# Layer 0's last half group of the down projection by block products, and a later place for the last square root's preparation

## The chip, the cores and the metric

The kernel runs on one core of a Trainium2 chip. Times are device microseconds (us) of one execution of the whole program. The engines are called as in the profile: PE (matrix multiplication; PEld are its weight loads), DVE (the vector engine), ACT (the activation engine), POOL, and SP, which here only issues DMAs.

## The reference

Two layers of a decoder trunk over 512 positions with a width of 1024. Each layer mixes (attention, convolution and RWKV heads between an input and an output projection) and then has a squared-ReLU MLP. The change lies in the MLP of layer 0 and in the end of the MLP of layer 1:

```python
D_MODEL = 1024; SEQ = 512; DEPTH = 2; D_FF = 4 * D_MODEL

def rms_norm(x, g):
    y = x * lax.rsqrt(jnp.mean(x * x, axis=-1, keepdims=True) + NORM_EPS)
    return y * g

for l in range(DEPTH):
    h = rms_norm(x, norm_mix_g[l])
    ...                                   # mixing, ends in x = x + mixed @ w_out[l]
    h = rms_norm(x, norm_mlp_g[l])
    x = x + jnp.square(jax.nn.relu(h @ w_mlp_up[l])) @ w_mlp_down[l]
return rms_norm(x, final_norm_g)
```

## The kernel before

**Layout.** x is kept transposed in eight tiles x[0] to x[7] of 128 x 512 (features on partitions, positions along the row). Every product is made in three passes: each operand is split into a rounded part (hi) and a remainder (lo), and hi x hi, hi x lo and lo x hi are summed. The hi part is a cast on ACT, the lo part a subtraction on DVE (lines 348 and 349 for weights of a plain product, 1583 and 1584 for those of a block product).

**The MLP.** It has 32 hidden tiles of 128 x 512, kept as pairs (hi, lo) in `mids` by `kept()` (lines 1406 to 1414), in two rings `mh` and `ml` of ten places each. The first four come from plain products (`up`), the other 28 from 14 calls of `two()`, each of which makes two hidden tiles by a block scheme. The down projection takes the hidden tiles in groups h = 0 to 7 of four, and each group in two halves of four output tiles: `down(h, range(0, 4))` and `down(h, range(4, 8))`. In the loop of lines 1694 to 1701 one half group follows each `two()`, so that it lags behind; after the loop the halves of group 6 are done and the two halves of group 7 are left, which lines 1702 to 1704 do with no `two()` between them.

**The two ways of a half group.** `down()` (lines 1659 to 1683) asks the list `DN_QUADS` (line 184), by layer, of pairs (h, half).

- Plain: for each of the four output tiles j, 4 hidden tiles x 3 passes = 12 matmuls of 512 columns into one accumulator, then one addition into x[j]. The weights of j are one load of 256 KB, one cast and one lo part. In layer 0 the group h = 7 then calls `norm_tile(j)` for j < 6, which accumulates the squares of x[j] for the next layer's norm (a square on ACT, line 384; from j = 1 on an addition into `accm` on DVE, line 385).
- Block products, `quad()` (lines 1577 to 1657): the four output tiles are taken as two pairs (j, j + 1). The weights of a pair are seen as 2 x 2 blocks (output tile j or j + 1, even or odd hidden tile), the hidden tiles as 2 x 2 blocks (even or odd tile, left or right half of the positions), and the product is made with seven block products in place of eight, each of 2 hidden tiles x 3 passes = 6 matmuls of 256 columns, 84 for the half group. For this, sums and differences of weights (lines 1618 to 1622) and of hidden tiles are needed, and the results are combined (lines 1638 to 1657). Products on accumulators pa, pb, pc appear in the profile as qa, qb and qc. The seven are issued in steps: first the two of the unsummed weights `w0` for both pairs, then the two of `s12`, then the two of `s34`, and at last the one of `w22`.

The sums of hidden tiles are made by `turn_blocks(h, k, b1, b2)` (lines 1560 to 1575), once for each two hidden tiles of a group (k = 0, 1): four differences on DVE, a cast on ACT and a lo part on DVE for two of them, then two smaller casts and lo parts for the other two. It is called in the loop right after the half group of that round (lines 1699 to 1701), and only for groups of which `DN_QUADS` has a half. It writes the tiles `dhi` and `dlo` of its k, and the right halves of `acts[2k]` and `acts[2k + 1]`, the MLP's input tiles (ahif, alof in the profile), which nothing else reads any more. All groups share these places, so in layer 0, whose list has both halves of the groups 2, 4 and 6, the groups between them go plain (group 1 has one half by block products).

**Buffers.** Weights of plain products and the unsummed ones of block products share the tags `raw`, `whi` and `wlo` with three places each, taken in turn (`Pool`, lines 243 to 257). The sums of weights go through the tiles s2 and s4 (one place each) and `shi`, `slo` (five each). The tag `c0` (two places) holds both the intermediate tiles of `turn_blocks` and the results c0 of `quad`.

**Order of the work.** The mixing stage of each layer is issued in an order written out by hand (`ORDER`). In the MLP, the order of instructions on each engine is set at compile time by a scheduler, from the order of the program and from what is ready; each engine then runs its own list in order. Layer 1's written order begins with products of its input projection (pj), which read the scaled tiles of x (ahim, alom; made for j < 6 by `scaled`, lines 391 and 392, and for the last two by `entry`, lines 426 and 427), and then has pssm, small matmuls that sum the accumulated squares `accm` over the features.

**The end of the kernel.** In layer 1 the last group goes through `last_group()` (lines 473 to 569), which also makes the final norm. Its root is a Sqrt activation (line 511). Line 480 issues a small Sqrt on a constant column, which makes ACT load its table.

Of the kernel before, what the change touches and what calls it, by code (L numbers as in the profile page):

```python
# [10 lines left out]
F32 = mybir.dt.float32  # L11
F32R = mybir.dt.float32r
# [168 lines left out]

N_ONE = 4

DN_QUADS = (((1, 0), (2, 0), (2, 1), (4, 0), (4, 1), (6, 0), (6, 1)), ((1, 0), (2, 0), (2, 1), (4, 0), (4, 1), (6, 0), (6, 1)))

WHOLE = 2
PT = 1
# [86 lines left out]
def tile_trunk(ctx: ExitStack, tc: tile.TileContext, xT, wts, prm_d, cst_d, lora_d, gup_d, lam_d, fin_d, hd_d, out):  # L274
# [198 lines left out]
    def last_group(fp, wbase, mids):  # L473
# [3 lines left out]
        mine = mids[-4:]  # L477
        acc = wp.tile([P, S], F32, tag="acc", bufs=1, name="accF")

        act.activation(cp.tile([P, NB], F32, tag="rr", bufs=2, name="rrF")[:, :1], ones1, AF.Sqrt)  # L480

        def group(j, home=None):
            return weights(wbase + NG_IN + NG_OUT + NG_UP + 8 * g + j, 4, NK, home=home)
# [87 lines left out]
    for l in range(L):  # L571
# [826 lines left out]
        with ExitStack() as mx:  # L1398
# [161 lines left out]
            def turn_blocks(h, k, b1, b2):  # L1560

                a = fp.tile([P, 2, H], F32, tag="c0", bufs=2, name=f"ta{l}_{h}_{k}")
                b = fp.tile([P, 2, H], F32, tag="c0", bufs=2, name=f"tb{l}_{h}_{k}")
                dve.tensor_tensor(a[:, 0], b1[:, H:], b1[:, :H], ALU.subtract)
                dve.tensor_tensor(a[:, 1], b2[:, H:], a[:, 0], ALU.subtract)
                dve.tensor_tensor(b[:, 0], b2[:, H:], b1[:, H:], ALU.subtract)
                dve.tensor_tensor(b[:, 1], b2[:, :H], a[:, 1], ALU.subtract)
                hi, lo = [fp.tile([P, 2, H], F32R, tag=f"d{p}{k}", name=f"d{p}{l}_{h}_{k}") for p in ("hi", "lo")]
                act.copy(hi, a)
                dve.tensor_tensor(lo, a, hi.bitcast(F32), ALU.subtract)  # L1570
                for i in range(2):
                    turned[i, k] = hi[:, i], lo[:, i]
                    vhi, vlo = turned[2 + i, k] = [t[:, H:] for t in acts[2 * k + i]]
                    act.copy(vhi, b[:, i])
                    dve.tensor_tensor(vlo, b[:, i], vhi.bitcast(F32), ALU.subtract)

            def quad(h, half):
# [15 lines left out]
                        pe.matmul(pt, wlo, ahi, start=False, stop=last and i == 1, skip_group_check=True)  # L1593

                blk = lambda d, q: lambda i: [t[:, q * H:(q + 1) * H] for t in mids[4 * h + 2 * i + d]]
                trn = lambda q: lambda i: turned[q, i]

                def add(j, q, pt):
                    dve.tensor_tensor(x[j][:, q], pt, x[j][:, q], ALU.add)
# [28 lines left out]
                for step in ((0, 1), (2, 3), (5, 4), (6,)):  # L1628
                    for j, w0, s12, s34, w22, (pa, pb, pc) in ab:
                        n = f"{l}_{h}_{j}"  # L1630
                        for c in step:
# [7 lines left out]
                            elif c == 2:  # L1639
                                product(pb, s12, (0, 1), trn(0), True, False)  # L1640
                                keep["p5", j] = copied("p5", pb, n)
                            elif c == 3:
                                product(pa, s12, (2, 3), trn(1), False, False)
                                keep["u2", j] = copied("u2", pa, n)
                            elif c == 5:
                                product(pb, s34, (2, 3), blk(1, 1), False, True)
                                c0 = keep["c0", j]
                                dve.tensor_tensor(c0[:, right], pb, keep["u2", j], ALU.add)
                                add(j, slice(0, S), c0)
                            elif c == 4:  # L1650
                                product(pa, s34, (0, 1), trn(2), False, False)
                                c1 = copied("c1", pa, n)
                                dve.tensor_tensor(c1, c1, keep["p5", j], ALU.add)  # L1653
                                add(j + 1, right, c1)
                            else:
                                product(pa, w22, (0, 1), trn(3), False, True)
                                add(j + 1, left, pa)

            def down(h, js):

# [115 lines left out]
```

## Time and profile before

| | us |
|---|---|
| median of 3 runs | 1225.97 |
| lowest and highest of them | 1225.78, 1226.85 |
| the profiled execution | 1225.8 |
| its span, from first to last instruction | 1224.0 |
| PE busy in it | 1213.5 |
| DVE busy | 1038.7 |
| ACT busy | 765.2 |
| POOL busy | 307.0 |

Times within the profile count from the start of the span. The stage around the change, layer 0's last block product to layer 1's first norm sums, lies between about 560 and 620 us. In rows of the timeline the columns are start, length, engine, line, operation, output and inputs, shapes and count; what stands in square brackets is the time that the engine was idle before, and what it waited for. Records of one engine can overlap by some 0.1 us, since an instruction starts before the last has quite ended.

### The profile page before, as it was taken

The numbers are of one execution on the slowest core, as the hardware profiler recorded it, in microseconds if no ns is written. First come the engines' busy times: TensorE is split into PE (matmuls) and PEld (weight loads), VectorE is DVE, ScalarE is ACT, GpSimd is POOL, SyncE is SP. The second block draws the span as 40 slices with busy tenths as digits, with TensorE's granted clock in tenths as the row PEclk, the third lists the DMA queues.
The fourth block names the chain that finished last, engine by engine and source line by source line (L and its number), as shares of the span: only waits on it lengthen the run. The fifth ranks groups of instructions, "written<-read, shape, count | busy, mean of one in ns | idle before, by whom it ended". The sixth has DMA issues, their size and how long they took to land.

```text
span 1224.0 us, 27303 instructions
## 1 busy us (share of the span) xinstructions
PE 1213.5 (99%) x10242; PEld 1070.0 (87%) x10242; DVE 1038.7 (85%) x2214; ACT 765.2 (63%) x1678; POOL 307.0 (25%) x446
## 2 busy tenths in 40 slices
PE   9999999999999999999999999999999999999997
PEld 7888788888999999989888888888889999999997
DVE  6787888878899998989866777887798999899895
ACT  7785655558476655646575656464675666465565
POOL 2364636341100010000026455464211000101001
PEclk9999999999999999999999999999999999999999
DMA  6533334126645473631235243232455556546112
GB/s 222 163 94 96 114 88 112 54 86 181 164 125 161 129 188 96 184 86 53 78 114 160 84 128 113 88 82 71 151 152 150 142 133 169 138 130 180 54 54 86
DMA packets 95508, 148.51 MB, mean 121 GB/s; under 512 B 22544, under 2 KB 26384, under 8 KB 95376
## 3 DMA queue, kind: packets, MB, share of 16 engines
q1 hardware_dynamic: 87168, 132.39, 34.5%
q0 software_dynamic: 7488, 13.63, 7.4%
q8 instruction: 80, 1.31, 0.4%
q10 hardware_dynamic: 720, 0.75, 0.2%
q14 instruction: 52, 0.43, 0.1%
HBM read 137.56 MB, written 9.18 MB: 120 GB/s over the span
## 4 chain that ended last, share of the span: by engine, by line
PE 92%; DVE 4%; ACT 2%; issue 1%; DMA 1%; POOL 0%; SPq 0%; POOLq 0%; ACTq 0%; DVEq 0%
PE pj L287 23%; PE dn L287 14%; PE pa L287 13%; PE po L287 8%; PE qa L287 7%; PE pb L287 7%; PE pc L287 3%; PE qb L287 3%; PE qc L287 2%; PE dnF L287 2%; PE sc L287 1%; PE ptt L292 1%; PE pg L287 1%; PE pyy L287 1%; DVE tlo L1469 1%
## 5 line engine op out<-in xcount | busy, mean ns | idle before, releaser
L697 POOL TENSOR_TENSOR wlo<-raw,whi 128x512 fp32r<-128x512 f32 x84 | 112.4, 1338 | 261.5 <-ACT whi L685 228.1
L287 PE MATMUL pj<-ahim,whi 128*128 128x512 f32 x392 | 156.9, 400 | 0.0
L287 PE MATMUL pj<-ahim,wlo 128*128 128x512 f32 x392 | 156.6, 399 | 0.0
L287 PE MATMUL pj<-alom,whi 128*128 128x512 f32 x392 | 156.0, 398 | 0.0
L1480 POOL DMA_DIRECT2D s<-wts x52 | 45.7, 879 | 433.1 <-DVE c1q L1653 52.8
L685 ACT CAST whi<-raw 128x512 fp32r<-128x512 f32 x142 | 87.7, 618 | 72.3 <-PE pj L287 24.5
L1494 ACT CAST shi_p<-s 128x512 fp32r<-128x512 f32 x112 | 69.6, 622 | 51.8 <-PE pa L287 29.8
L287 PE MATMUL dn<-ml,whi 128*128 128x512 f32 x256 | 99.9, 391 | 0.4 <-DVE ml L1413 0.4
L287 PE MATMUL dn<-mh,whi 128*128 128x512 f32 x256 | 99.9, 391 | 0.0
L287 PE MATMUL dn<-mh,wlo 128*128 128x512 f32 x256 | 99.3, 390 | 0.0
L287 PE MATMUL pa<-thi,shi_p 128*128 128x256 f32 x336 | 95.2, 283 | 0.0
L287 PE MATMUL pa<-tlo,shi_p 128*128 128x256 f32 x336 | 94.8, 282 | 0.0
L287 PE MATMUL pa<-thi,slo_p 128*128 128x256 f32 x336 | 94.3, 281 | 0.0
L1495 DVE TENSOR_TENSOR slo_p<-s,shi_p 128x512 fp32r<-128x512 f32 x112 | 76.3, 689 | 13.8 <-ACT shi_p L1494 13.0
L287 PEld LDWEIGHTS pj<-alom,whi 128*128 128x128 f32 x392 | 73.9, 189 | 14.0 <-issue 0.5
L287 PEld LDWEIGHTS pj<-ahim,wlo 128*128 128x128 f32 x392 | 73.9, 188 | 13.8 <-issue 0.2
L287 PEld LDWEIGHTS pj<-ahim,whi 128*128 128x128 f32 x392 | 73.9, 189 | 13.6 <-issue 0.3
L1494 ACT CAST shi_p<-raw 128x512 fp32r<-128x512 f32 x84 | 52.0, 621 | 30.5 <-PE pb L287 12.7
L287 PEld LDWEIGHTS pa<-thi,shi_p 128*128 128x128 f32 x336 | 63.0, 187 | 0.9 <-ACT u L1538 0.5
L287 PEld LDWEIGHTS pa<-thi,slo_p 128*128 128x128 f32 x336 | 63.7, 190 | 0.0
L287 PEld LDWEIGHTS pa<-tlo,shi_p 128*128 128x128 f32 x336 | 63.2, 188 | 0.0
L1495 DVE TENSOR_TENSOR slo_p<-raw,shi_p 128x512 fp32r<-128x512 f32 x84 | 57.7, 688 | 5.1 <-ACT shi_p L1494 4.5
(648 smaller groups left out, 4002.2 us busy)
## 6 DMA issues: line engine op xcount, KB each, us to landing
raw<-wts SPq DMA_DIRECT2D x307, 256.0 KB, 3.0
rawq<-wts SPq DMA_DIRECT2D x56, 256.0 KB, 2.9
s<-wts SPq DMA_DIRECT2D x52, 256.0 KB, 3.6
s<-wts POOLq DMA_DIRECT2D x52, 256.0 KB, 4.6
qs<-dqhi SPq DMA_DIRECT2D x24, 128.0 KB, 3.3
ks<-dkhi SPq DMA_DIRECT2D x24, 128.0 KB, 3.5
x<-xT SPq DMA_DIRECT2D x8, 256.0 KB, 5.3
dqhi<-qhi SPq DMA_DIRECT2D x6, 256.0 KB, 3.3
```

The costliest lines, as they stand in the source:

```text
L287: ins = nc.tensor.matmul(*a, **k)
L292: ins = nc.tensor.transpose(*a, **k)
L685: yield act.copy(hi[:, k0:k1], raw[:, k0:k1])
L697: yield eng.tensor_tensor(lo[:, k0:k1], raw[:, k0:k1], hi[:, k0:k1].bitcast(F32), ALU.subtract)
L1469: dve.tensor_tensor(lo[:, u], t, hi[:, u].bitcast(F32), ALU.subtract)
L1480: pool.dma_start(t.rearrange("p k c -> p (k c)"), of[1], accum_op=ALU.add)
L1494: act.copy(hi, src)
L1495: dve.tensor_tensor(lo, src, hi.bitcast(F32), ALU.subtract)
```

## The change

1. `DN_QUADS` of layer 0 gets the pair (7, 0): the first half of the last group goes by block products. The second half, (7, 1), stays plain.
2. With this `turn_blocks` is called for group 7 too, in the last two rounds of the loop. The call for k = 0 comes while `quad(6, 1)` still has to read the sums of group 6. So it gets places of its own: two places of each of the rings mh and ml (`own`, `ring`). The call for k = 1 writes the shared places, behind `quad(6, 1)`. `turned` is indexed by the group as well.
3. `quad()` calls `norm_tile` for the two tiles of a pair after its last product if h is 7.
4. The small Sqrt of `last_group` reads one column of the last hidden tile, which the last `two()` makes, instead of a constant.

```diff
-DN_QUADS = (((1, 0), (2, 0), (2, 1), (4, 0), (4, 1), (6, 0), (6, 1)), ...
+DN_QUADS = (((1, 0), (2, 0), (2, 1), (4, 0), (4, 1), (6, 0), (6, 1), (7, 0)), ...
...
-        act.activation(cp.tile([P, NB], F32, tag="rr", bufs=2, name="rrF")[:, :1], ones1, AF.Sqrt)
+        act.activation(cp.tile([P, NB], F32, tag="rr", bufs=2, name="rrF")[:, :1], mine[-1][0][:, :1].bitcast(F32), AF.Sqrt)
...
-                hi, lo = [fp.tile([P, 2, H], F32R, tag=f"d{p}{k}", name=f"d{p}{l}_{h}_{k}") for p in ("hi", "lo")]
+                ring = lambda n: [fp.tile([P, 2, H], F32R, tag="m" + p[0], bufs=RING, name=f"d{p}{l}_{h}_{k}_{n}") for p in ("hi", "lo")]
+                own = h == 2 * N_KG - 1 and k == 0
+                hi, lo = ring(0) if own else [fp.tile([P, 2, H], F32R, tag=f"d{p}{k}", name=f"d{p}{l}_{h}_{k}") for p in ("hi", "lo")]
+                if own:
+                    more = ring(1)
                 act.copy(hi, a)
                 dve.tensor_tensor(lo, a, hi.bitcast(F32), ALU.subtract)
                 for i in range(2):
-                    turned[i, k] = hi[:, i], lo[:, i]
-                    vhi, vlo = turned[2 + i, k] = [t[:, H:] for t in acts[2 * k + i]]
+                    turned[h, i, k] = hi[:, i], lo[:, i]
+                    vhi, vlo = turned[h, 2 + i, k] = [t[:, i] for t in more] if own else [t[:, H:] for t in acts[2 * k + i]]
...
-                trn = lambda q: lambda i: turned[q, i]
+                trn = lambda q: lambda i: turned[h, q, i]
...
                                 product(pa, w22, (0, 1), trn(3), False, True)
                                 add(j + 1, left, pa)
+                                if h == 2 * N_KG - 1:
+                                    norm_tile(j, f"m{l + 1}")
+                                    norm_tile(j + 1, f"m{l + 1}")
```

More of the change, by code (lines that the diff above doesn't have):

```diff
@@ L182 @@
 N_ONE = 4
-DN_QUADS = (((1, 0), (2, 0), (2, 1), (4, 0), (4, 1), (6, 0), (6, 1)), ((1, 0), (2, 0), (2, 1), (4, 0), (4, 1), (6, 0), (6, 1)))
+DN_QUADS = (((1, 0), (2, 0), (2, 1), (4, 0), (4, 1), (6, 0), (6, 1), (7, 0)), ((1, 0), (2, 0), (2, 1), (4, 0), (4, 1), (6, 0), (6, 1)))
 WHOLE = 2
```

## The prediction

> **What bounds the kernel now.** I read the page first: the busy shares, the slices, and the chain that ended last.
>
> ```profile
> span 1224.0 us, 27303 instructions
> PE 1213.5 (99%) x10242; PEld 1070.0 (87%) x10242; DVE 1038.7 (85%) x2214; ACT 765.2 (63%) x1678; POOL 307.0 (25%) x446
> DVE  6787888878899998989866777887798999899895
> PE 92%; DVE 4%; ACT 2%; issue 1%; DMA 1%; POOL 0%; SPq 0%; POOLq 0%; ACTq 0%; DVEq 0%
> ```
>
> PE is busy all the time and the chain runs over it. But DVE stands at nine tenths in several slices, and the change adds DVE work. So I looked at the stage that is changed: the chain in order of time around the end of layer 0.
>
> ```profile
> 578.44 0.71 PE qa L287 x6
> ...
> 586.29 2.15 PE qa L287 x18
> 588.44 21.91 PE dn L287 x96
> 610.35 4.08 PE pj L287 x18
> 614.43 0.56 PE pssm L287 x16
> ```
>
> From 578.44 to 588.44 runs quad(6, 1), the last block product; then 96 plain matmuls, both halves of down(7); then layer 1 begins with 18 matmuls of its projection and with pssm, the sums over x that its norm needs. PE never waits in this stretch. The busy time of each engine in the same stretch (columns: PE, PEld, DVE, ACT, POOL, each with its count, then clock, DMA share, GB/s):
>
> ```profile
> core 0: us, PE busy (x) PEld busy (x) DVE busy (x) ACT busy (x) POOL busy (x), PEclk, DMA share, GB/s
> 553.80:560.80 7.00, 7.00 (x61) 7.00 (x60) 6.93 (x17) 4.69 (x10) 0.00 (x0) 1.00 0.21 76
> 560.80:582.90 22.10, 22.10 (x186) 21.98 (x186) 22.04 (x49) 15.60 (x37) 0.00 (x0) 1.00 0.12 37
> 582.90:588.44 5.54, 5.54 (x48) 5.54 (x47) 3.63 (x10) 2.43 (x7) 0.00 (x0) 1.00 0.14 47
> 588.44:599.40 10.96, 10.96 (x49) 8.86 (x49) 8.41 (x15) 6.01 (x11) 0.00 (x0) 1.00 0.31 96
> 599.40:610.35 10.95, 10.95 (x50) 9.08 (x49) 9.67 (x16) 7.11 (x12) 0.00 (x0) 1.00 0.29 97
> 610.35:613.23 2.88, 2.88 (x15) 2.37 (x14) 2.88 (x5) 2.33 (x5) 2.32 (x2) 1.00 0.02 8
> ```
>
> Here DVE has next to no idle time from 553.80 to 582.90 and little after it. PE sets the pace, with DVE just behind. This is the view on which I build.
>
> **The change on PE.** It removes 48 matmuls of 512 columns, half of the 96 that took 21.91: 10.96 us. It adds 84 of 256 columns, as quad(6, 1) did in 588.44 - 578.44 = 10.00 us. If nothing else mattered, PE would gain 0.96 us, 0.08% of the time. A measurement of this kernel tells about 0.2% (2.45 us) from no change, so this alone could not be seen.
>
> **The change on DVE.** Its price per instruction is the distance between starts, not the length of a record:
>
> ```profile
> 543.70 0.68 DVE L1570 TENSOR_TENSOR dlo<-ta,dhi 128x512 fp32r<-128x512 f32 x1
> 544.30 0.42 DVE L1575 TENSOR_TENSOR alof<-tb,ahif 128x256 fp32r<-128x256 f32 x1
> 544.63 0.69 DVE L1584 TENSOR_TENSOR wlo_0a<-rawq,whi_0a 128x512 fp32r<-128x512 f32 x1
> ```
>
> 512 elements take 0.60 us (543.70 to 544.30), 256 take 0.33. From the code, each of the two pairs of a quad has four instructions of 512 (three low parts, one addition into x) and ten of 256 (four block sums, one low part, five sums of results): 4 x 0.60 + 10 x 0.33 = 5.70, so 11.40 for quad(7, 0). The plain half had four low parts and four additions: 8 x 0.60 = 4.80, which go. turn_blocks was not called for h = 7 before and is now called twice, each time with six instructions of 256 and one of 512: 2.58, together 5.16. Net 11.40 - 4.80 + 5.16 = 11.76 us more on DVE.
>
> Where can it go? turn_blocks(7, 0) reads hidden tiles 28 and 29, whose last square ends at 560.81 (first row below); everything has to be done before pssm, which reads the accumulated squares of all eight tiles of x, and half of x now comes out of the quad. That join is in the other rows:
>
> ```profile
> 560.18 0.63 ACT L1422 ACTIVATE m<-m 128x512 f32<-128x512 f32 x1
> ...
> 612.54 0.68 DVE L442 TENSOR_TENSOR accm<-accm,sqm 128x512 f32<-128x512 f32 x1
> 613.14 0.74 DVE L427 SCALAR_TENSOR_TENSOR alom<-x,prm,ahim 128x512 fp32r<-128x512 f32 x1
> ...
> 614.36 0.63 PE L287 MATMUL pssm<-ones,accm 128*64 128x1 f32 x16
> ```
>
> The last accumulation ends at 613.22 and PE comes at 614.36: 1.14 us of slack. Between 560.80 and 613.23 DVE was idle for 0.06 + 1.91 + 2.55 + 1.28 + 0 = 5.80 us by the table. A record is 0.09 longer than the place it takes, so about eight gaps hide 0.7 more: 5.8 to 6.5. Even if every gap is filled, the join moves by 11.76 - 6.5 - 1.14 = 4.1 to 11.76 - 5.8 - 1.14 = 4.8 us. I take 4.5. PE's 0.96 does not count here, since PE waits for DVE either way.
>
> Can the gaps be filled, and does DVE run without new ones? Two rows show the largest:
>
> ```profile
> 584.98 0.42 DVE L1648 TENSOR_TENSOR c0q<-qb,u2q 128x256 f32<-128x256 f32 x1 [1.88 <-PE qb L287]
> 592.49 0.69 DVE L1681 TENSOR_TENSOR x<-dn,x 128x512 f32<-128x512 f32 x1 [2.21 <-PE dn L287]
> ```
>
> In both DVE waited for PE's next result with nothing else to do. The pushed-back turn_blocks(7, 0) fills the first, the preparation of the quad the second, so I count them as filled. New gaps come from hand-offs. Until now a two() always lay between two quads, and gave the preparation its lead:
>
> ```profile
> 548.31 0.69 DVE L1681 TENSOR_TENSOR x<-dn,x 128x512 f32<-128x512 f32 x1 [1.70 <-PE dn L287]
> ...
> 567.55 0.62 ACT L1583 CAST whi_4a<-rawq 128x512 fp32r<-128x512 f32 x1
> 571.20 0.69 DVE L1584 TENSOR_TENSOR wlo_4a<-rawq,whi_4a 128x512 fp32r<-128x512 f32 x1
> ```
>
> whi_4a was cast 10.9 us ahead of its use at 578.44. The three places of whi are taken in turn: the first weight of quad(7, 0) gets that of whi_4d, which quad(6, 1) reads nearly to its end at 588.44. So its cast, its low part and PE's third matmul now follow one another, behind turn_blocks(7, 1), whose later parts wait for the same end, in the DVE queue. Behind that queue also stand the quad's sums and the norm work of x[0] to x[3], which was spread over 592 to 602 and now comes in one lump. I add 0.7 us for such hand-offs, from nothing (all hidden) up to 2.0 (one full gap like those above, again).
>
> ACT gets about 7 us more (ten casts of 0.62 and six of about 0.4, six copies of 0.37, less four casts of 0.62), against over 18 idle in the table: it does not decide. DMA is the same, four loads of 256 KB on SP either way; POOL has nothing there. The ring places are free: they held hidden tiles 20 to 23, whose readers, down(5), ended with the addition at 548.31.
>
> **The Sqrt at the end.** Now:
>
> ```profile
> 900.89 1.28 ACT L480 ACT_TABLE_LOAD   x1
> 902.19 0.20 ACT L480 ACTIVATE rrF<-ones 128x1 f32<-128x1 f32 x1
> ...
> 905.94 0.50 PE L287 MATMUL dn<-ml,whi 128*128 128x512 f32 x1 [0.26 <-DVE ml L1413]
> ```
>
> The load holds ACT for 1.4 us behind the first ups of layer 1, and PE then waits 0.26 for a hidden tile. Reading the last hidden tile puts it behind this row:
>
> ```profile
> 1182.08 0.62 ACT L1412 CAST mh<-m 128x512 fp32r<-128x512 f32 x1
> 1182.60 0.64 ACT L1603 COPY p1q<-qa 128x256 f32<-128x256 f32 x2
> ...
> 1183.61 0.72 PE qa L287 x6
> ```
>
> The copies at 1182.60 free the sums that PE needs again at 1183.61. Placed before them, the 1.4 us cost up to 0.75; behind them, in ACT's gaps, nothing. So the edit is worth between -0.26 and +0.5; I take -0.2, since it comes last in program order. [...]
>
> **Sum.** 4.5 + 0.7 - 0.2 = 5.0 us. The profiled execution took 1225.8 us, 1.8 more than its span, and the median is 1225.97: 1226.0 + 5.0 = 1231.0. Ends of the likeliest case: 4.1 + 0 - 0.26 = +3.8 and 4.8 + 2.0 + 0.5 = +7.3, so 1229.8 to 1233.3.
>
> **Rivals.** (1) DVE's extra work does not reach the join. For it: PE is the bound by share, and not all DVE work before the join is needed there: three low parts of layer 1's weights (0.60 each) and the low parts of x[6] and x[7] (a record of 0.74, less 0.09) could be queued behind it. If they are, 4.5 falls by up to 3.1; with hand-offs hidden and the Sqrt's -0.2 the time is 1227.2. If in addition the squares were queued early enough, only PE's terms remain: -0.96 - 0.26, 1224.8. It decides when less than about 2.5 us of the 11.76 remain uncovered. Against it: layer 1's beginning is an order written out, which has these parts ahead of the last accumulation. [...] Chance 0.18.
>
> (2) PE's wait comes in one piece and its clock falls.
>
> ```profile
> 1216.99 1.16 PE L287 MATMUL prbF<-cst,rsxF 128*128 128x128 f32 x8 [1.21 <-DVE rsxF L516]
> ...
> 1216.00:1218.00 2.00, 1.01 (x8) 0.97 (x8) 0.98 (x6) 0.08 (x1) 0.00 (x0) 1.00 0.48 157
> 1218.00:1220.00 2.00, 0.15 (x2) 0.00 (x0) 1.81 (x6) 0.37 (x1) 1.31 (x2) 0.67 0.40 131
> 1220.00:1222.00 2.00, 0.00 (x0) 0.00 (x0) 0.00 (x0) 0.00 (x0) 0.09 (x1) 0.50 1.02 332
> ```
>
> A wait of 1.21 us left the granted clock at 1.00; after PE's last work it was 0.50 within some two us. If PE waits much longer than 1.2 us ahead of the quad, its next work could run at half speed. The rows do not show for how long; I take 3 us of work, thus +3, between nothing (the lost time lies under DVE's backlog) and the plain half's whole 10.95. That gives 1234.0. It decides if the stall comes as one; several short ones would not do it. [...] Chance 0.12.
>
> (3) The order that the scheduler makes of everything behind the change comes out better by luck, by more than 2.45 us. The terms give at most 1.2 us, so nothing in the profile speaks for it. 1223. Chance 0.04. That the change does not do what it says is no case of its own: the list DN_QUADS is what down() asks.
>
> **How the numbers follow.** My forecast has 0.66. Slower by over 0.2% is the forecast and rival 2: 0.78. Within 0.2% is rival 1: 0.18. Faster is rival 3: 0.04. The range must leave out no more than 2 in 10: from 1226.8, within rival 1, to 1235.0, past rival 2.
>
> **What would show it.** In the changed profile: DVE without gaps from about 554 to 618; PE with waits at the head of the quad and ahead of pssm, which starts near 619.4 in place of 614.4; the quad longer than 10 us; from pssm on both kernels alike, shifted. The Sqrt's load between 1182 and 1190, and no wait near 906. I am wrong if pssm starts before 617, if DVE keeps gaps in the stage, or if layer 1 gives the shift back.

## The result, and the profile after

The changed kernel takes 1236.93 us (median of 6 runs, 1233.61 to 1239.35); the kernel before took 1226.41 beside it (6 runs, 1225.78 to 1227.58). The ratio is 1.0078, with a 95% interval from 1.0064 to 1.0092: 10.5 us slower, where 5.0 were forecast. The direction was right, the size was not. The profiled execution took 1236.99.

The page of the changed kernel, the same lines as before:

```profile
span 1235.2 us, 27415 instructions
PE 1218.7 (99%) x10278; PEld 1074.0 (87%) x10278; DVE 1050.8 (85%) x2248; ACT 771.1 (62%) x1696; POOL 305.6 (25%) x446
PE 87%; DVE 7%; ACT 2%; issue 1%; DMA 1%; POOL 0%; SPq 0%; POOLq 0%; DVEq 0%; ACTq 0%
```

DVE was busy for 1038.7 us and now is for 1050.8: 12.1 more, close to the 11.76 of the prediction. PE fell from 92% of the chain to 87%, DVE rose from 4% to 7%. Where this lies is seen in the chain around the end of layer 0, in order of time:

```profile
555.64 0.61 DVE slo_0c L1588
...
594.61 0.62 DVE slo_0b L1588
595.27 0.75 PE qb L287 x4
...
605.62 10.26 PE dn L287 x45
616.51 2.07 DVE alom L392 x2
618.58 0.61 DVE wlo L697
619.23 5.54 PE pj L287 x16
624.78 0.56 PE pssm L287 x16
```

Before, this chain ran over PE without a break. Now nearly all its steps from 555 to 595 are on DVE, then the quad and the plain half on PE, and a second piece of DVE, the end of which (wlo, the low part of layer 1's first weight) lets PE go on at 619.23. The busy times in the stretches that the prediction used (PE, PEld, DVE, ACT, POOL, clock, DMA):

```profile
582.90:588.44 5.54, 5.54 (x49) 5.54 (x48) 5.54 (x14) 3.35 (x11) 0.00 (x0) 1.00 0.31 98
588.44:599.40 10.96, 8.23 (x49) 7.34 (x49) 10.28 (x27) 6.27 (x14) 0.00 (x0) 0.84 0.15 49
599.40:610.35 10.95, 10.95 (x70) 9.76 (x69) 10.06 (x21) 8.64 (x18) 0.00 (x0) 1.00 0.14 48
```

The old gaps of DVE are filled, as forecast, but new ones have come: 0.68 and 0.89 us in the second and third row, where it waits for products of the new quad and once for a cast, and 2.0 us in all from 560.8 to the last accumulation, against 5.80 before. In the second row two more things are new: PE was busy for only 8.23 of 10.96, and its granted clock had a mean of 0.84. What PE waited for, with the total, the count and the longest (the first three are the longest of the stage, the last row has two small ones):

```profile
PE pj L287 <- DVE wlo L697: 2.9, 1, 2.9
PE qb L287 <- ACT shi_0b L1587: 1.4, 1, 1.4
...
PE qa L287 <- DVE wlo_0a L1588: 1.1, 1, 1.1
...
PE dn L287 <- DVE ml L1413: 0.5, 2, 0.3
```

The clock by the microsecond, behind the two waits in the quad and behind the one at the join:

```profile
593.00:594.00 1.00, 0.00 (x0) 0.00 (x0) 1.00 (x4) 0.66 (x2) 0.00 (x0) 1.00 0.00 0
...
596.00:597.00 1.00, 1.00 (x7) 1.00 (x6) 1.00 (x4) 0.47 (x2) 0.00 (x0) 0.50 1.03 375
...
599.00:600.00 1.00, 1.00 (x10) 1.00 (x9) 0.42 (x1) 1.00 (x3) 0.00 (x0) 0.86 0.00 0
...
618.00:619.00 1.00, 0.00 (x0) 0.00 (x0) 1.00 (x2) 0.00 (x0) 0.26 (x1) 1.00 0.00 0
...
620.00:621.00 1.00, 1.00 (x4) 0.81 (x3) 1.00 (x3) 0.00 (x0) 0.00 (x0) 0.50 0.65 186
```

While PE is idle the clock still reads 1.00, and so it does for the first 1.6 or 0.5 us after work is back; then it is at 0.50, for 3.4 us each time (595.9 to 599.3, and 619.8 to 623.2). The 16 matmuls of pj that took 5.54 us in the chain took 3.94 in a kernel where the clock stayed at 1.00 behind the same kind of wait (without the sums of group 7, below).

The two rows on which the prediction had built its join, behind the low part that PE waits for:

```profile
618.50 0.68 DVE L697 TENSOR_TENSOR wlo<-raw,whi 128x512 fp32r<-128x512 f32 x1
...
620.97 0.68 DVE L442 TENSOR_TENSOR accm<-accm,sqm 128x512 f32<-128x512 f32 x1
...
624.71 0.63 PE L287 MATMUL pssm<-ones,accm 128*64 128x1 f32 x16
```

In the kernel before this low part was made in this row:

```profile
605.95 0.68 DVE L697 TENSOR_TENSOR wlo<-raw,whi 128x512 fp32r<-128x512 f32 x1
```

Counted from the start of quad(6, 1), which is 578.27 before and 578.96 now, the last accumulation ends after 34.95 and 42.69 us (+7.74), and pssm starts after 36.09 and 45.75 (+9.66). These two lengths are the measure in all that follows, since they leave out what differs ahead of the stage from one execution to the next. From pssm to pssf, layer 1's next norm sums, both kernels take the same: 266.30 and 266.44. So the loss is made in this one stage and is not given back. The rest of the 11.2 us between the two profiled executions is 0.69 ahead of the stage and 0.85 behind pssm. The three kernels without block products in group 7 and without its work on POOL differ by as much among themselves: quad(6, 1) starts at 577.2 to 578.3, and 609.6 to 611.6 us lie behind the start of pssm.

### The profile page after: what moved, and what is told of

Same layout as the page of the kernel before. It is cut to its first block, busy times and chain, and to the rows that moved or that the text cites. A ratio compares the mean times of both kernels' runs of the same rounds, so it can differ in the third digit from the quotient of the medians.

```text
span 1235.2 us, 27415 instructions
## 1 busy us (share of the span) xinstructions
PE 1218.7 (99%) x10278; PEld 1074.0 (87%) x10278; DVE 1050.8 (85%) x2248; ACT 771.1 (62%) x1696; POOL 305.6 (25%) x446
## 3 DMA queue, kind: packets, MB, share of 16 engines
q8 instruction: 80, 1.31, 0.4%
HBM read 137.56 MB, written 9.18 MB: 119 GB/s over the span
## 4 chain that ended last, share of the span: by engine, by line
PE 87%; DVE 7%; ACT 2%; issue 1%; DMA 1%; POOL 0%; SPq 0%; POOLq 0%; DVEq 0%; ACTq 0%
PE pj L287 22%; PE dn L287 13%; PE pa L287 13%; PE po L287 8%; PE pb L287 6%; PE qa L287 6%; PE pc L287 3%; PE qb L287 3%; PE dnF L287 2%; PE qc L287 1%; PE sc L287 1%; PE ptt L292 1%; PE pg L287 1%; PE pyy L287 1%; DVE tlo L1469 1%
## 5 line engine op out<-in xcount | busy, mean ns | idle before, releaser
L287 PE MATMUL dn<-ml,whi 128*128 128x512 f32 x240 | 93.9, 391 | 0.5 <-DVE ml L1413 0.5
L287 PE MATMUL dn<-mh,whi 128*128 128x512 f32 x240 | 93.8, 391 | 0.2 <-ACT mh L1412 0.2
L287 PE MATMUL dn<-mh,wlo 128*128 128x512 f32 x240 | 93.2, 390 | 0.0
L1494 ACT CAST shi_p<-raw 128x512 fp32r<-128x512 f32 x84 | 52.0, 622 | 29.9 <-PE pb L287 12.1
```

Source lines behind the costliest of these rows:

```text
L287: ins = nc.tensor.matmul(*a, **k)
L1494: act.copy(hi, src)
```

## The experiments

All kernels start from the changed one unless it says otherwise, and differences are taken against the kernel before on the same chip. A summary first; "DVE" is the net work that the change adds there by the prediction's prices, and the lengths count from the start of quad(6, 1):

| kernel | DVE, us | last accumulation | pssm | against before, us | ratio, 95% |
|---|---|---|---|---|---|
| before | 0 | 34.95 | 36.09 | | |
| Sqrt alone | 0 | 34.93 | 36.07 | -0.9 | 0.9985 to 1.0002 |
| sums alone, unread | 5.16 | 35.00 | 36.13 | -0.7 | 0.9986 to 1.0002 |
| no sums | 6.60 | 36.47 | 37.93 | +1.65 | 1.0004 to 1.0021 |
| half of the sums | 9.18 | 39.05 | 42.09 | +5.4 | 1.0033 to 1.0057 |
| changed | 11.76 | 42.69 | 45.75 | +10.5 | 1.0064 to 1.0092 |
| changed, again | 11.76 | 42.87 | 45.93 | +9.8 | 1.0062 to 1.0100 |
| block products alone | 11.76 | 42.85 | 45.88 | +8.6 | 1.0055 to 1.0081 |
| both halves | 18.36 | 48.59 | 51.83 | +15.75 | 1.0111 to 1.0142 |
| PE kept busy at the join | 11.76 | 43.59 | 45.04 | +8.4 | 1.0050 to 1.0074 |
| PE kept busy at both places | 11.76 | 41.84 | 44.14 | +8.1 | 1.0050 to 1.0075 |
| first low part on POOL | 11.16 | 43.40 | 43.45 | +9.0 | 1.0056 to 1.0083 |
| both of the last two | 11.16 | 40.63 | 42.96 | +6.3 | 1.0038 to 1.0065 |

My theory was that the amount of DVE work sets the join. The first rival: something else in the new quad does, above all PE's waits and the clock behind them. The second: layer 1's order of work at the join.

**The Sqrt alone**, in the kernel before.

```diff
-        act.activation(cp.tile([P, NB], F32, tag="rr", bufs=2, name="rrF")[:, :1], ones1, AF.Sqrt)
+        act.activation(cp.tile([P, NB], F32, tag="rr", bufs=2, name="rrF")[:, :1], mine[-1][0][:, :1].bitcast(F32), AF.Sqrt)
```

> The kernel before with the Sqrt edit alone. My prediction gave it -0.26 to +0.5 us: the load leaves its place behind the first ups of layer 1, the wait of 0.26 us near 906 goes, and nothing new waits if the load falls into one of ACT's gaps. I expect 0.2 us less than before, not to be told from it. If the loss of the change lay in this edit, this kernel would be slower by several us.

Measured 1226.86, no different from before. The load went to 1183.94, behind the copies, and cost nothing there. But PE's wait near 906 stayed, and was longer:

```profile
906.53 0.50 PE L287 MATMUL dn<-ml,whi 128*128 128x512 f32 x1 [0.58 <-DVE ml L1413]
```

So the table load had not caused it: DVE comes late with ml there by itself. The -0.2 of the prediction had its place wrong and is too small to be seen.

**The block products alone** (the Sqrt's line as in the kernel before).

```diff
-        ... mine[-1][0][:, :1].bitcast(F32), AF.Sqrt)
+        ... ones1, AF.Sqrt)
```

> The changed kernel with the Sqrt at its old place, so the block products alone. If they carry the whole loss: about 10.5 us above before, within 0.5 us of the changed kernel. If the Sqrt edit carries a part, this one is faster than the changed kernel by that part.

1236.38, ratio 1.0068 (1.0055 to 1.0081): the whole loss belongs to the block products and their sums.

**PE kept busy at the join**: 14 matmuls that nobody reads, in two tiles behind the last plain product, to keep the clock up during the wait for wlo.

```diff
-                    mm3(pt, weights(...), mids[4 * h:4 * h + 4], 4)
+                    ws = list(weights(...))
+                    mm3(pt, ws, mids[4 * h:4 * h + 4], 4)
...
+                if h == 2 * N_KG - 1:
+                    for a in range(2):
+                        idle2 = psum("at", 2, f"warm{a}")
+                        for _ in range(7):
+                            pe.matmul(idle2, ws[3][1], mids[-1][0], start=True, stop=True)
```

> The changed kernel with 14 needless matmuls of 512 columns (3.2 us) on PE between the last plain product and layer 1's first one, where the changed kernel's PE waits for 2.9 us and then ran at a granted clock of 0.50. Their sums are read by nobody. Theory clock: the wait lets the clock fall, and 16 matmuls took 5.5 us in place of 3.6; kept busy, PE gets the 1.9 us back, some 1235.0. Theory that PE's late start alone counts and the clock does nothing: no gain, or the needless work comes on top, 1237 to 1238.

The wait went, and 18 pj took 4.18 us where 16 had taken 5.54, but pssm came only 0.71 earlier, and the time is 1236.18, between the two theories: the ratio of 1.0062 is not clear of the 1.0068 of the kernel above on the same chip. The clock still fell in the quad, and here it stayed at 0.50 for 6.8 us (592.2 to 599.1), with the last accumulation at 43.59.

**Layer 1's first low part on POOL**, to take it out of DVE's queue. The first string names the engine of each low part of layer 1 (x for DVE, y for POOL), the second is its written order; both go on as before.

```diff
-      "xyxyyxxxyyxxyyxyxxyxyyxyyyyyyxxx
+      "yyxyyxxxyyxxyyxyxxyxyyxyyyyyyxxx
...
-         "d3 w e x q d e w q y d w
+         "d3 w e y q d e w q y d w
```

> The changed kernel with the low part of layer 1's first weights made on POOL, which is idle there, in place of DVE; no other instruction of DVE changes its place. Theory queue place: this low part stands behind six scaled tiles on DVE, which come in one lump after the block products, and PE waits 2.9 us for it; on POOL it is ready before PE comes, the clock stays up, and the join waits only for the last squares on DVE: 3 to 3.6 us less than the changed kernel, some 1233.5. Theory that only the amount of DVE work counts: 0.6 us less, one instruction, 1236.3.

A miss: 1236.73 where 1233.5 was expected. The wait for wlo went, pssm came 2.3 us earlier, and now waited for the next thing on DVE:

```profile
618.47 1.76 DVE L442 TENSOR_TENSOR accm<-accm,sqm 128x512 f32<-128x512 f32 x1
...
621.49 0.63 PE L287 MATMUL pssm<-ones,accm 128*64 128x1 f32 x16 [2.38 <-DVE accm L442]
```

The join itself behaved as the theory said: pssm follows the last accumulation by 0.05 us, where 3.06 lay between them in the changed kernel. But behind that wait the clock fell (0.50 from 622.4 to 625.8), after pssm this time, and took a part of the gain back. And an accumulation of 0.68 us took 1.76 while POOL worked beside it; this comes back below.

**The changed kernel again**, for the spread of such a profile.

No line differs.

> The changed kernel again, beside before and the kernels below on one chip, since two chips differed by some us: about 10 us above before.

1237.23; the two lengths agree with the first profile within 0.2 us.

**Without the sums of group 7**: quad(7, 0) reads the sums of group 6, so this part of the computation is left out.

```diff
-                trn = lambda q: lambda i: turned[h, q, i]
+                trn = lambda q: lambda i: turned[min(h, 6), q, i]
-                if any(q[0] == hk[0] for q in DN_QUADS[l]):
+                if hk[0] < 7 and any(q[0] == hk[0] for q in DN_QUADS[l]):
```

> The changed kernel without the two calls of turn_blocks for group 7; its block products read the sums of group 6 in their place, so that PE, the weights and the additions do the same work and 5.2 us of DVE (and 2.8 of ACT) are left out. Theory amount of DVE work: the last accumulation comes 5.2 us earlier, and with it the join, which PE then reaches at nearly the same time; 2 to 4 us above before. Theory hand-offs: the waits at the head of the block products (the first weight's cast behind the last read of the group before) stay, and so do the falls of the clock; only 1 to 2 us are gained, 8 us above before.

1229.11, 1.65 us above before, a little less than the 2 to 4 expected: without 5.16 us of DVE work some 8 of the 10 us are gone, the clock stays at 1.00, and PE has one long wait, still for wlo:

```profile
613.65 0.50 PE L287 MATMUL pj<-ahim,wlo 128*128 128x512 f32 x1 [1.65 <-DVE wlo L697]
...
617.52 0.63 PE L287 MATMUL pssm<-ones,accm 128*64 128x1 f32 x16
```

So the order at the join can be seen here without the slow clock: pssm starts 1.46 us behind the end of the last accumulation.

**The sums alone**: the half stays plain, the sums of group 7 are made and nobody reads them.

```diff
-DN_QUADS = (... (6, 0), (6, 1), (7, 0)), ...
+DN_QUADS = (... (6, 0), (6, 1)), ...
-                if any(q[0] == hk[0] for q in DN_QUADS[l]):
+                if hk[0] == 7 and l == 0 or any(q[0] == hk[0] for q in DN_QUADS[l]):
```

> The kernel before with the two calls of turn_blocks for group 7 and with the Sqrt edit, but with the plain half group: 5.2 us more on DVE between 560 and 613, which had 5.8 to 6.5 idle there, and nothing else. The sums are read by nobody. Theory amount of DVE work: it fits, at most 0.5 us above before. Theory that any work in this stretch of DVE moves the join: 3 to 5 us above.

1226.76. The same 5.16 us that carry most of the loss cost nothing by themselves: they lie in DVE's gaps. It is the sum with the quad's 6.60 that overflows.

**PE kept busy at both places**: as above, and 8 more unread matmuls behind the first two products of quad(7, 0).

```diff
                                 product(pc, w0, (1, 3), blk(1, 0), True, True)
+                                if h == 2 * N_KG - 1 and j == 0:
+                                    for a in range(2):
+                                        idle2 = psum("rp", 4, f"warmq{a}")
+                                        for _ in range(4):
+                                            pe.matmul(idle2, w0[1][:, 3], mids[-1][0], start=True, stop=True)
```

> The changed kernel with the 14 needless matmuls ahead of layer 1 and 8 more of 512 columns (1.8 us) behind the first pair's first products, where PE waited 1.4 us for the first summed weights and the clock fell some us later. Theory clock: it stays at 1.00 in both places, the quad gets the 1.7 us back that half speed cost there, of which DVE shows as a gap of 0.7; with the join's 1.9 us the kernel is 2 to 3 us faster than the changed one. Theory that DVE hides what happens in the quad: not faster than the kernel with the 14 alone (8.4 us above before).

The clock is 1.00 all through the stage, yet the time is 1235.57, 1.7 us below the changed kernel on the same chip, where 2 to 3 were expected. The last accumulation comes 0.85 us earlier than in the changed kernel: about so much the half clock in the quad had put on it. At the join the unread matmuls took the place of what they saved.

**Both turn_blocks on POOL**, which is idle in the stage (0.00 in the table of before); all seven subtractions go to eng as the one shown.

```diff
             def turn_blocks(h, k, b1, b2):
+                eng = pool if h == 2 * N_KG - 1 else dve
...
-                dve.tensor_tensor(lo, a, hi.bitcast(F32), ALU.subtract)
+                eng.tensor_tensor(lo, a, hi.bitcast(F32), ALU.subtract)
```

> The changed kernel with the element work of both turn_blocks of group 7 moved from DVE to POOL, seven instructions each (no work is left out, PE and ACT do the same). If the amount of work on DVE decides, DVE is relieved of 5.2 us as in the kernel without these turn_blocks, and pssm comes about 38 to 40 us after the start of quad(6, 1), against 45.8 in the changed kernel: 1229 to 1232 us. POOL needs about 2 x (6 x 0.72 + 1.3) = 11.2 us for the two calls by its rows at L529 and L697, and the second call's last parts stand behind quad(6, 1), so PE may wait about 1 us in the quad for them. Rival: POOL beside DVE makes DVE's instructions longer (the two alom beside a POOL instruction took twice as long), or POOL's slower chain holds up PE, so that the quad's waits grow as much as the join's shrink: 1235 to 1239 us.

1238.77, ratio 1.0082 (1.0065 to 1.0098): the theory missed, and the time is in the range of its rival. DVE has seven instructions fewer, twice over, and the time did not fall. PE now waited for 2.4 us up to 575, ahead of the quads, where nothing had waited before.

**Both halves of group 7 by block products**, the double dose of the quad.

```diff
-DN_QUADS = (... (6, 1), (7, 0)), ...
+DN_QUADS = (... (6, 1), (7, 0), (7, 1)), ...
-                                if h == 2 * N_KG - 1:
+                                if h == 2 * N_KG - 1 and j < NK - LATE:
```

> The changed kernel with the second half of group 7 by block products as well: on PE again 48 matmuls of 512 out (10.96 us) and 84 of 256 in (10.0 us); on DVE 11.40 us in, 4.80 out, +6.6 us, and no further turn_blocks, since both halves read the same sums. If DVE is the pace from 555 to the join, which the changed kernel has filled without gaps, all 6.6 us reach the join: 1243 to 1246 us, some 17 above the kernel before. If the cost lay in the first handing over from quad to quad alone (the wait for the free weight place and for turn_blocks), a second one with its sums already there costs little: 1236 to 1239 us. If PE's own products set the time, it is 1 us faster than the changed kernel: 1236.

1243.12, ratio 1.0126: 15.75 us above the kernel before on its chip, some 6 above the changed one by the ratios, in the range of the DVE theory. The last accumulation moves by 5.90 us more and pssm by 6.08, for 6.6 of added work.

**Relief by POOL, in two steps**: turn_blocks(7, 0), the low parts of the plain half and layer 1's first low part on POOL (its two strings as above); then turn_blocks(7, 1) too (without the condition on k).

```diff
+                eng = pool if h == 2 * N_KG - 1 and k == 0 else dve
...
-            (pool if a and lean[0] else dve).tensor_tensor(lo[:, :n], raw[:, :n], hi[:, :n].bitcast(F32), ALU.subtract)
+            (pool if a and lean[0] or g in lowpool else dve).tensor_tensor(lo[:, :n], raw[:, :n], hi[:, :n].bitcast(F32), ALU.subtract)
...
+    lowpool = set(NG_IN + NG_OUT + NG_UP + 24 + j for j in range(4, 8))
```

> The changed kernel with some of DVE's work put on POOL, which is idle in the stage: turn_blocks(7, 0) whole, the four low parts of the weights of the plain half down(7, 1), and layer 1's first low part. DVE is relieved of 2.58 + 4 x 0.60 + 0.60 = 5.6 us, two of the three pieces right ahead of the join. If the amount on DVE and PE's two long waits (with the half clock behind them) are the whole of the loss, the join comes about 6 to 8 us earlier than in the changed kernel: 1229 to 1231 us. If POOL's instructions slow DVE's or come late themselves (a low part takes about 1.3 us there against 0.60), 1232 to 1236 us.

> As the one before, with turn_blocks(7, 1) on POOL too: DVE is relieved of 5.16 + 2.4 + 0.6 = 8.2 us of the 11.8 that the change adds. If the amount on DVE decides, the join is within 2 us of the kernel before and PE's 0.96 us counts for something: 1226 to 1229 us, the first form of the change that does not lose. If POOL's chain for turn_blocks(7, 1), whose last parts stand behind quad(6, 1), holds up the quad, PE waits there for about 1 to 3 us: 1229 to 1233 us.

Both missed: 1237.16 and 1236.03, ratios 1.0077 (1.0062 to 1.0093) and 1.0067 (1.0052 to 1.0082). The stage itself is shorter, pssm after 41.04 and 40.29, but quad(6, 1) starts at 582.16 and 580.33, behind the same new wait of 2.4 us (578.27 before).

**POOL alone**: the kernel with the unread sums, and these made on POOL. DVE's work is that of the kernel before.

```diff
+                eng = pool if h == 2 * N_KG - 1 else dve
...
-                dve.tensor_tensor(lo, a, hi.bitcast(F32), ALU.subtract)
+                eng.tensor_tensor(lo, a, hi.bitcast(F32), ALU.subtract)
```

> The kernel with the plain half and the late Sqrt, and with both turn_blocks of group 7 made on POOL though nobody reads them: DVE has exactly the work of the kernel before, POOL some 11 us more. On DVE the same sums cost nothing (ratio 0.9994). If POOL takes time from DVE while both work, DVE falls behind by some 3 to 5 us at the first call near 567, PE waits about 2.4 us for the low part of shi_p near 573 as in the three runs with these sums on POOL, and its clock falls to one half there: 1229 to 1232 us. Rival: POOL works beside DVE at no cost, and the waits in those runs came from the quad: 1226.5 to 1228 us.

1231.30, ratio 1.0039 (1.0027 to 1.0051), where the same sums on DVE were free: the time and the wait came as said, but the clock stayed at 1.00 in the profiled execution. The timeline of this kernel, DVE and POOL:

```profile
564.82 0.68 DVE L1605 TENSOR_TENSOR x<-c0q,x 128x512 f32<-128x512 f32 x1
...
566.64 1.22 DVE L1605 TENSOR_TENSOR x<-c0q,x 128x512 f32<-128x512 f32 x1
...
568.04 1.31 POOL L1576 TENSOR_TENSOR dlo<-ta,dhi 128x512 fp32r<-128x512 f32 x1 [0.73 <-ACT dhi L1575]
568.12 0.41 DVE L1605 TENSOR_TENSOR x<-qa,x 128x256 f32<-128x256 f32 x1
568.46 1.18 DVE L1605 TENSOR_TENSOR x<-c1q,x 128x256 f32<-128x256 f32 x1
...
572.64 0.39 PE L287 MATMUL pa<-thi,shi_p 128*128 128x256 f32 x1 [2.39 <-ACT p L1526]
```

The addition x<-c0q,x takes 0.68 us alone (first row) and 1.22 beside POOL. x<-c1q,x took 1.18 in the middle of POOL's 1.31 (0.42 at 567.80 in the changed kernel, where POOL does nothing), while x<-qa,x, which reads one operand from an accumulator, kept its 0.41. So here DVE's instructions with both operands in SBUF took longer beside POOL's; what causes it, these rows do not show. In 564 to 572 DVE got through 14 instructions, against 19 in the kernel before, and was busy for 7.91 us all the same. An idle POOL was therefore no help for this DVE work. The slowed DVE explains the new wait of the three kernels above, since PE's wait of 2.4 us is there without any block product; how much of their 8.7 to 11.4 us goes back to it beyond the 4.7 of this kernel was not separated.

**The order and the clock together**: the first low part on POOL (both strings as above), 8 unread matmuls in the quad and 6 behind the plain half.

```diff
-         "d3 w e x q d e w q y d w
+         "d3 w e y q d e w q y d w
...
+                                        for _ in range(4):
+                                            pe.matmul(idle2, w0[1][:, 3], mids[-1][0], start=True, stop=True)
...
+                        for _ in range(3):
+                            pe.matmul(idle2, ws[3][1], mids[-1][0], start=True, stop=True)
```

> The changed kernel with layer 1's first low part on POOL and with needless matmuls that nobody reads at the two places where PE waits long, 8 behind the first two products of quad(7, 0) and 6 behind the plain half. If the loss is the amount of DVE work and, on top, the order at the join and the half clock, then with the two of them away only the amount is left: the last accumulation comes 6 to 7 us later than in the kernel before, of which 1.1 is slack, so pssm some 42 us after the start of quad(6, 1) (36.1 before, 45.8 changed), and 1231.5 to 1233.5 us. Rival: the order and the clock are not what costs, or POOL's low part slows the DVE beside it by as much as it relieves it: 1235 to 1237 us.

1232.94, ratio 1.0052, in the range; the last accumulation comes 5.7 us later than before, where 6 to 7 were expected. The clock is 1.00 all through the stage, and PE's waits in it are down to these:

```profile
PE qa L287 <- DVE wlo_0a L1588: 1.1, 1, 1.1
PE pj L287 <- POOL wlo L697: 0.3, 1, 0.3
PE dn L287 <- DVE x L1603: 0.3, 1, 0.3
```

Each of the two remedies alone gained at most 2.2 us by the ratios (1.0081 to 1.0063 on one chip; for the low part nothing, 1.0070 beside 1.0068 of the block products alone). Together they take off some 3.2 (1.0078 - 1.0052, from different chips), and 2.8 of the stage (45.75 - 42.96). What is left, 6.3 us, is not the amount on DVE alone: the last accumulation, 5.68 later, accounts for 4.5 beyond the slack of 1.14, and pssm stands 2.3 behind it. In these 2.3 are up to 1.4 us of unread matmuls (6 x 0.228) and PE's wait for POOL, whose low part of some 1.3 us lasted 3.66 among two-operand instructions of DVE that followed one another without a gap:

```profile
616.19 3.66 POOL L697 TENSOR_TENSOR wlo<-raw,whi 128x512 fp32r<-128x512 f32 x1 [4.29 <-ACT whi L685]
```

**Half of the sums**: turn_blocks(7, 1) left out; for these two hidden tiles the sums of group 6 are read, so this part of the computation is left out.

```diff
-                trn = lambda q: lambda i: turned[h, q, i]
+                trn = lambda q: lambda i: turned[min(h, 7 - i), q, i]
-                if any(q[0] == hk[0] for q in DN_QUADS[l]):
+                if hk != (7, 1) and any(q[0] == hk[0] for q in DN_QUADS[l]):
```

> The changed kernel without turn_blocks(7, 1): for those two hidden tiles quad(7, 0) reads the sums of group 6, so that part of the computation is left out; 2.58 us less on DVE, half of what the kernel without both calls left out. If the loss goes in proportion to DVE's work, it lies halfway between that kernel (+1.7 us) and the changed one (+10): 1232.5 to 1234. If it comes in one step, when a wait of PE becomes long enough for the half clock, it lies at one of the ends: 1229 to 1230.5, or 1236 to 1237.

1231.98, 5.4 us above before: about halfway between 1.65 and 10, half a microsecond below the range. The quad has no long wait any more, the join has the same one as the changed kernel (2.92 us for wlo) and the half clock behind it.

**No sums, and the first low part on POOL**: the best that the change could be if its sums were free (group 7's sums are left out as above, and the first low part's strings are those above).

```diff
-                trn = lambda q: lambda i: turned[h, q, i]
+                trn = lambda q: lambda i: turned[min(h, 6), q, i]
...
-         "d3 w e x q d e w q y d w
+         "d3 w e y q d e w q y d w
```

> The kernel without both turn_blocks of group 7 (sums of group 6 read in their place, so part of the computation is left out) and with layer 1's first low part on POOL: the best that the change could be if its sums cost nothing. The wait of 1.65 us for that low part goes: 1227 to 1228 us, no different from the kernel before; PE's 0.96 us does not show, since the 6.6 us more of DVE work in the quad fill the gaps. If PE sets the time once DVE is relieved, 1226 us or less. If POOL slows the DVE beside it, 1229 us as without this edit.

A miss: 1229.55, ratio 1.0024 (1.0013 to 1.0035), as without this edit. The wait for wlo went, but POOL's low parts met the last accumulation:

```profile
613.31 1.76 DVE L442 TENSOR_TENSOR accm<-accm,sqm 128x512 f32<-128x512 f32 x1
...
615.12 0.63 PE L287 MATMUL pssm<-ones,accm 128*64 128x1 f32 x16 [1.35 <-DVE accm L442]
```

A wait of 1.35 us, and the clock then was 0.50 from 617 to 620. So even with free sums the change did not gain in this form, and no version that I tried beats the kernel before.

## Why the forecast had the direction right and the size wrong

**PE's terms held.** 84 matmuls came for 48, and the saving of 0.96 us shows nowhere, since PE waits for DVE.

**The price of the DVE work held.** The prediction let the last accumulation move by the work, less 5.8 to 6.5 us of gaps, plus 0.7 for hand-offs. With 6.15 for the gaps that is 1.15, 3.73, 6.31 and 12.91 us for the four doses of the table (6.60, 9.18, 11.76 and 18.36). Measured are 1.52, 4.10, 7.74 and 13.64. Two doses lie 0.37 above, the double one 0.73; the changed kernel lies 1.43 above, of which about 0.85 is the half clock in its quad. The term for hand-offs was thus short by some 0.4 to 0.7 us: right in kind, a little small. It shows on DVE itself as new gaps, above all 0.68 us ahead of 599.11 and 0.51 ahead of 600.04, both while PE ran at half clock.

**The step that failed is the join.** The prediction took the last accumulation as the one gate of pssm, with 1.14 us of slack. That was read from the kernel before, in which layer 1's first low part was made at 605.95, long ahead of its use. In the changed kernel DVE's backlog pushes it behind the last of the six scaled tiles (alom), to 618.50, and the 16 products pj behind it end later than the accumulation. At the full clock, with the 3.87 us from the first of them to pssm in the kernel without sums (613.65 to 617.52), pssm would come at 619.23 + 3.87 = 623.10, 1.45 us behind the accumulation's end of 621.65. Two kernels bear this out: without sums pssm starts 1.46 us behind the accumulation at the full clock, and with the first low part on POOL 0.05. The prediction named these low parts only as work that might be queued behind the join, not as a second gate ahead of it.

**The clock was a rival and should have been a term.** Rival 2 gave the fall of the clock 3 us and a chance of 0.12. It happened, twice: about 0.85 us on the accumulation and 5.54 - 3.94 = 1.6 at the join. That the two together come near the 3 us is luck: one fall costs about half of that or less, and the rival counted one. Its condition was wrong too. I held that several short waits would not do it; in the quad waits of at most 1.4 us did. And I had looked for it at the quad alone, while the longest wait came at the join, where the forecast itself expected PE to wait. A forecast in which PE waits for DVE by several us contains the rival's condition; the two belonged in one sum.

Together: 7.74 - 1.14 = 6.6 us by the accumulation, 1.45 by the order at the join, 1.6 by the clock there, 9.65 in all, against pssm's 9.66. That the order and the clock hold pssm back by 3.06 us behind the accumulation is shown by the kernel with the first low part on POOL; what the program could gain by it is less, since each taken away by itself brought out the other or the next wait, and both taken away brought 2.8 us of stage, most of it by an earlier accumulation (40.63 against 42.69).

**The other rivals fell.** That DVE's work would not reach the join (0.18) is refuted by the four doses; pssm before 617, named as a sign for it, is not there. Gaps on DVE, named as another sign of being wrong, are there, 2.0 us in the stage, but they are hand-offs, in which DVE waits for the new quad's products and a cast, while all its added work still came ahead of pssm. The direction owes nothing to luck. Of the signs of the forecast, PE's two places of waiting, a longer quad and a layer 1 that gives nothing back came as said; DVE had the gaps, pssm came at 624.71 in place of 619.4, and the Sqrt's load came behind the copies as wanted, but at 1193.80, since all behind the stage is shifted. The wait near 906 did not go with the Sqrt.

Open is how much idle time of PE within one step of the clock's grid is enough to lower it, as the last section tells. Whether layer 1's first low part, made on DVE ahead of the scaled tiles, would have saved its part without POOL's cost was not tried.

## What to carry to other kernels

Where two engines are both near full in a stage, count the added work against the gaps of the second one there, and then list every operation of that engine that the next stage needs: the slack read at one of them in the old order says nothing of the others once a backlog reorders them. If the forecast makes PE wait by more than a microsecond, put the slower clock behind the wait into the sum from the start, with a chance: here it came behind a wait of 1.35 us already, one fall cost 0.85 to 1.6 us, and some waits of 1.4 to 2.4 us were without one. And before work is moved to an idle engine, look in the trace at how long the neighbour's instructions take while both work.

## What the runs showed of the hardware that was not expected

DVE's two-operand instructions on SBUF took longer beside POOL's: 0.68 us became 1.22, and 1.76 in the accumulations, while instructions that read an accumulator kept 0.41. POOL's low part, with a median of 1.29 us in the kernel before, became 3.66 beside such instructions of DVE. The kernel before has a row of this at its join, which I had not read so:

```profile
610.64 1.43 POOL L697 TENSOR_TENSOR wlo<-raw,whi 128x512 fp32r<-128x512 f32 x1 [86.74 <-ACT whi L685]
611.43 1.19 DVE L697 TENSOR_TENSOR wlo<-raw,whi 128x512 fp32r<-128x512 f32 x1
```

The changed kernel has it ahead of the low part that PE waited for: two scaled tiles beside a POOL low part of 616.10 to 617.37, which took 0.66 us more than the two at 614.14 (1.41).

```profile
616.51 2.07 DVE L392 SCALAR_TENSOR_TENSOR alom<-x,prm,ahim 128x512 fp32r<-128x512 f32 x2
```

So 0.66 us of PE's wait of 2.9 come from this, and they delay the accumulation as well; the kernel before had lost 0.5 in the row at 611.43.

The granted clock fell to 0.50 after waits much shorter than I had assumed: after 1.35 us ahead of pssm, and after 1.1 and 1.4 within 4 us. It stayed there for 3.41 us each time, or for 6.83: behind the quad's waits with PE kept busy at the join (592.2 to 599.1), and at the join with both halves (621.2 to 628.1). But it did not follow from the length alone. The same wait of 2.4 us, pa for shi_p, left the clock at 0.50 for 3.4 us in two kernels (both turn_blocks on POOL, the first step of relief) and at 1.00 in two others (the second step of relief, POOL alone); a wait of 1.65 us left it at 1.00 in the kernel without sums; and the kernel with both halves kept 1.00 through waits of 1.0 and 1.4 us in its first quad.

The traces show what these cases have in common. Within an execution all changes of the clock lie on one grid of 3.413 us. In the changed kernel they are at 595.87, 599.29, 619.77, 623.18 and, after PE's last work, 1227.34: 1, 6, 1 and 177 steps apart. What followed a wait went with PE's idle time within one step of the grid:

| kernel and wait | PE idle, us, in the steps that the wait touches | clock in the step behind |
|---|---|---|
| both turn_blocks on POOL, 2.40 | 2.40 in one | 0.50 |
| first step of relief, 2.39 | 2.18, then 0.21 | 0.50 behind the 2.18 |
| second step of relief, 2.40 | 0.92, then 1.47 | 1.00 |
| POOL alone, 2.39 | 0.71, then 1.68 | 1.00 |
| changed, first quad, 1.10 and 1.38 | 1.13, then 1.61 | 0.50 behind the 1.61 |
| both halves, first quad, 1.05 and 1.38 | 0.99, then 1.47 | 1.00 |

In the stage, over all the traces, the clock was at 0.50 behind every step with 1.96 us of idle time or more and fell behind none with less than 1.35; between 1.35 and 1.68 it fell in some and not in others. (The 1.35 us are the wait ahead of pssm, and its 16 products of one column lie in the same step.) So for the waits of 2.4 us the outcome goes with their position on the grid, though no run varied the position alone. What decides between 1.35 and 1.7 us is open, and so is why two stretches lasted two steps.
